# A list scheduler that may leave VectorE and ScalarE idle for work due sooner, and plans with TensorE's clock

## The chip, the core and the metric

The kernel runs on one core of a Trainium2 chip. The metric is the device time of one execution in microseconds (us); less is better. Inputs, outputs and weights are float32 and lie in HBM; the program reads 598 MB and writes 2 MB. The core has five engines with a queue of instructions each: TensorE (PE in the profile) multiplies matrices, VectorE (DVE) and ScalarE (ACT) work element by element, GpSimd (POOL) does little here, and SyncE (SP) issues the loads. Within an engine instructions run in the order in which the program lists them; between engines they wait for each other through semaphores.

## The reference

Two layers of a transformer trunk over 256 tokens of width 2048. Both layers have the same frame, with `cond = silu(c)`:

```python
mod = (cond @ ada_w[i] + ada_b[i])[:, None, :]
sh1, sc1, g1, sh2, sc2, g2 = jnp.split(mod, 6, axis=-1)
h = _rms_norm(x, ln_mix_g[i]) * (1.0 + sc1) + sh1
# layer 0: y = _mla_mixer(h, ...), layer 1: y = _dsa_mixer(h, ...)
x = x + g1 * y
h = _rms_norm(x, ln_ffn_g[i]) * (1.0 + sc2) + sh2
x = x + g2 * _swiglu(h, ffn_w_gate_up[i], ffn_w_down[i])
```

The first mixer, MLA, has low-rank projections with a norm inside them, 16 heads with rotary embedding and a norm of each head's q and k, causal softmax attention and an output projection. The second, DSA, has full q, k and v projections, an indexer that selects 64 keys per query, and attention over those. The FFN has a hidden width of 5632. A root-mean-square norm is `x * rsqrt(mean(x * x) + eps) * g`.

## The kernel before

**Staging.** The 256 tokens stand as two tiles of 128 rows, `xs[0]` and `xs[1]`, in SBUF for the whole program. All weights are streamed from HBM in tiles of 128 x 1024 floats (0.5 MB), used once. Matrix products keep nearly full float32 precision by splitting each operand in a high and a low part: a weight tile `raw` lands, ScalarE writes its high part `whi`, VectorE writes `wlo = raw - whi`, and `mm3` makes three matmuls of each product into a PSUM tile `acc`. Three buffers each of `whi` and `wlo` and five of `raw` stand between the loads and TensorE, so that TensorE can go on for some microseconds only when VectorE is late with `wlo`.

**Modulation.** `cond @ ada_w` is a product with one row. It runs mostly on VectorE: for each of 16 slices of 128 rows, `ada_tiles` does `acc = raw * cond + acc` (tile names `araw` or `raw`, and `ada`). These are the longest VectorE operations beside `wlo`, and a `Stream` spreads them between the weight loads of whatever stage runs. At the start of the program the first layer's `sc1` and `sh1` are made this way in four chunks, with some of the slices on TensorE, while the input projection of MLA already runs on the chunks that are done.

**Norms.** `sumsq` squares on ScalarE and sums along the row (its elementwise result goes to a tile `junk` that nobody reads), and `rstd` computes the reciprocal root on VectorE as a chain of 11 tiny operations, each of which reads the result of the one before (`rs_h`, `rs_t`, `rs_g`, `rs_p`). `norm_stats` and `norm_group` use it for x (results `nv`, `nr`, `xn`), `lora` for the low-rank norms, and each of the eight head pairs of MLA for its q and k (`v8`, `r8`, printed as `r`). After a pair's chain come on VectorE `k_r` and `qs`, on ScalarE the scaling of `kv`, on TensorE the transposes and the scores, on VectorE the masked row maxima (`prob`, `mx`), on ScalarE the exponentials, on VectorE the reciprocal of the sum, on ScalarE the scaling of `prob`, and on TensorE the transposes of `prob` and the product with v.

**Who sets the order.** No line of the kernel issues directly. Every call is recorded as an `Op` with a duration from the table in `cost`, and `place` orders the whole program: it simulates the five engines (`run`), derives from the simulated schedule a due time for every operation (the time at which TensorE's next use of its result would be delayed), simulates again with these due times as priorities, eight times in all, and keeps the schedule with the shortest simulated span. TensorE keeps the order of the source, less an offset for code under `rec.boost`. `run` is greedy: of the operations that are ready when an engine becomes free it takes the one due first, and an engine is never left idle while any operation is ready. `issue` then lists the program in simulated order, and on the chip each engine follows its list.

**Memory.** `const` tiles live for the whole program. A tile with a tag takes one of the tag's buffers in turn, and its first use waits until the buffer's last holder is done (`link`).

## Time and profile before

| | us |
|---|---|
| median of 3 runs | 2390.15 (2389.46 to 2390.41) |
| the profiled execution | 2388.56 |
| its span from first to last instruction | 2386.8 |
| TensorE busy in it | 2299.2 |
| VectorE busy | 1703.9 |
| ScalarE busy | 1145.9 |

The profiled execution is one run with the profiler on; 1.76 us of it lie outside the span. Times inside the trace count from the span's start. By stages: 0 to about 180 is the start (modulation, first norm, input projection of MLA), to about 350 the MLA heads, to 427 the output projection, then the first FFN to 1178, the DSA mixer to 1639 and the second FFN to the end. TensorE's granted clock is given as a share of 2.4 GHz: 1.00 is that level and 0.50 is 1.2 GHz.

### The profile page before, as it was taken

The page shows a single profiled execution, that of the slowest core. Times are in us where ns is not written, and L with a number is a line of the kernel's source. Part 1 is how long each engine was busy: PE and PEld are TensorE (multiplying, and loading weights), DVE is VectorE, ACT ScalarE, POOL GpSimd, SP SyncE. Part 2 cuts the span into 40 slices and gives each one's busy share as a digit, 9 for nine tenths or more (in the row PEclk, how much of TensorE's full clock was granted, in tenths as well). Part 3 has the DMA queues.
Part 4 walks back from the last instruction along what each step waited for, and adds up shares of the span by engine and source line. Part 5 has one row for each costly group of instructions (what it writes and reads, how often), then busy time and mean ns, then how long its engine had stood idle before and what let it go on. Part 6 is the DMA issues. An engine that isn't in the chain of part 4 may idle for free.

```text
span 2386.8 us, 29405 instructions
## 1 busy us (share of the span) xinstructions
PE 2299.2 (96%) x10394; PEld 1866.2 (78%) x10394; DVE 1703.9 (71%) x2373; ACT 1145.9 (48%) x1740; POOL 31.6 (1%) x93
## 2 busy tenths in 40 slices
PE   6889989799999999999899999998999999999999
PEld 2467768688888888888778888887888888888887
DVE  7768979877787788888789666657676554455455
ACT  2248964644434443444455665655444344434443
POOL 1000000000000000000000000000000000000000
PEclk8889999999999999999999999999999999999999
DMA  9958978788899998999667677655887666666665
GB/s 359 337 181 301 336 259 275 262 301 309 300 322 314 314 309 309 324 306 304 227 203 230 195 227 224 200 177 177 290 280 243 193 192 191 189 193 193 187 190 162
DMA packets 278401, 601.87 MB, mean 252 GB/s; under 512 B 18804, under 2 KB 27088, under 8 KB 277998
## 3 DMA queue, kind: packets, MB, share of 16 engines
q1 hardware_dynamic: 277852, 599.97, 76.3%
q8 instruction: 81, 1.33, 0.2%
q14 instruction: 66, 0.54, 0.1%
q10 hardware_dynamic: 402, 0.04, 0.0%
HBM read 597.84 MB, written 2.10 MB: 251 GB/s over the span
## 4 chain that ended last, share of the span: by engine, by line
PE 85%; DVE 7%; ACT 4%; issue 3%; DMA 1%; SPq 0%; DVEq 0%; ACTq 0%
PE acc L398 78%; PE ms L398 7%; DVE ada L398 2%; DVE wlo L398 2%; ACT whi L398 1%; ACT prob L398 1%; DMA araw<-in_ada_w_dram 1%; ACT junk L398 1%; ACT hT L398 0%; DVE y L398 0%; ACT kv L398 0%; DMA raw<-in_ada_w_dram 0%; DVE hT L398 0%; DVE rs_g L398 0%; DVE hf L398 0%
## 5 line engine op out<-in xcount | busy, mean ns | idle before, releaser
L398 DVE TENSOR_TENSOR wlo<-raw,whi 128x1024 fp32r<-128x1024 f32 (+1 forms) x758 | 919.7, 1214 | 520.2 <-ACT whi L398 517.9
L398 PE MATMUL acc<-whi,hT 128*128 128x512 f32 (+1 forms) x4096 | 1282.0, 391 | 3.2 <-ACT hT L398 2.5
L398 ACT ACTIVATE whi<-raw 128x1024 fp32r<-128x1024 f32 (+1 forms) x758 | 797.8, 1054 | 1006.9 <-PE acc L398 922.2
L398 PEld LDWEIGHTS acc<-whi,hT 128*128 128x128 f32 x4096 | 769.4, 189 | 166.0 <-issue 5.8
L398 PE MATMUL acc<-wlo,hT 128*128 128x512 f32 (+1 forms) x2048 | 801.2, 391 | 3.0 <-DVE wlo L398 2.9
L398 PE MATMUL acc<-whi,oT 128*128 128x512 f32 x1920 | 600.2, 391 | 0.0
L398 PEld LDWEIGHTS acc<-wlo,hT 128*128 128x128 f32 x2048 | 386.4, 189 | 82.8 <-DVE wlo L398 4.8
L398 PEld LDWEIGHTS acc<-whi,oT 128*128 128x128 f32 x1920 | 360.9, 188 | 74.5 <-ACT whi L398 0.4
L398 PE MATMUL acc<-wlo,oT 128*128 128x512 f32 x960 | 375.4, 391 | 3.3 <-DVE wlo L398 3.3
L398 DVE SCALAR_TENSOR_TENSOR ada<-raw,condT,ada 128x1024 f32<-128x1024 f32 (+1 forms) x256 | 310.6, 1214 | 43.8 <-DMA raw<-in_ada_w_dram 41.6
L398 PEld LDWEIGHTS acc<-wlo,oT 128*128 128x128 f32 x960 | 180.7, 188 | 41.4 <-DVE wlo L398 4.5
L398 DVE SCALAR_TENSOR_TENSOR ada<-araw,condT,ada 128x512 f32<-128x512 f32 (+1 forms) x176 | 165.6, 941 | 11.6 <-ACT condT L398 6.7
L398 ACT ACTIVATE hT<-ms,modT,modT 128x256 fp32r<-128x256 f32 x64 | 33.8, 568 | 58.3 <-PE ms L398 31.7
L398 PE MATMUL ms<-ident,xn 128*128 128x128 f32 x144 | 29.3, 354 | 25.1 <-DVE rs_p L398 13.0
L398 PE MATMUL ms<-araw,condT 128*1 128x512 f32 x96 | 51.4, 675 | 1.7 <-ACT condT L398 1.7
L398 PEld LDWEIGHTS ms<-ident,xn 128*128 128x128 f32 x144 | 23.3, 189 | 30.2 <-ACT xn L398 12.3
L398 DVE TENSOR_TENSOR y<-acc,gB 128x512 f32<-128x512 f32 x64 | 42.1, 683 | 6.2 <-PE acc L398 6.2
L398 ACT ACTIVATE oT<-ms 128x512 fp32r<-128x512 f32 x60 | 35.7, 598 | 20.6 <-PE ms L398 18.2
L398 DVE TENSOR_TENSOR oT<-ms,oT 128x512 fp32r<-128x512 f32 x60 | 39.7, 683 | 7.4 <-ACT oT L398 7.3
L398 POOL MEMSET ada<- 128x1024 f32 (+1 forms) x30 | 23.6, 785 | 1388.4 <-PE ms L398 702.6
L398 ACT ACTIVATE prob<-prob,mx,qs 128x128 f32<-128x128 f32 (+1 forms) x64 | 34.2, 536 | 13.6 <-DVE mx L398 13.6
L398 DVE TENSOR_TENSOR x<-x,y 128x512 f32<-128x512 f32 x56 | 38.0, 684 | 0.4
(213 smaller groups left out, 995.9 us busy)
## 6 DMA issues: line engine op xcount, KB each, us to landing
raw<-in_ffn_w_gate_up_dram SPq DMA_DIRECT2D x352, 512.0 KB
raw<-in_ada_w_dram SPq DMA_DIRECT2D x240, 512.0 KB
raw<-in_ffn_w_down_dram SPq DMA_DIRECT2D x176, 512.0 KB
araw<-in_ada_w_dram SPq DMA_DIRECT2D x144, 512.0 KB
raw<-in_dsa_w_in_dram SPq DMA_DIRECT2D x114, 512.0 KB
raw<-in_mla_w_out_dram SPq DMA_DIRECT2D x32, 512.0 KB
raw<-in_dsa_w_out_dram SPq DMA_DIRECT2D x32, 512.0 KB
raw<-in_mla_w_in_dram SPq DMA_DIRECT2D x16, 512.0 KB
```

The source lines that it names most:

```text
L398: op.call(*[real(a) for a in op.args], **{k: real(v) for k, v in op.kw.items()})
```

## The change

Five edits. (1) `run` may pass over a ready operation on VectorE or ScalarE. If the operation that it would start now has a rival that becomes ready within 260 ns, and also within 0.4 of this operation's own duration, and is due more than 500 ns sooner, then the engine stays idle until the rival is ready. (2) The simulated TensorE gets a clock: an operation takes its columns at 1.2 GHz if fewer than 3072 columns streamed in the simulated tick before (`pace`). (3) The elementwise result of `sumsq` has three buffers in place of one. (4) To make room, `vrows` moves into a buffer of the tag `hf`, which the rotary angles use too. (5) The rotary tables of MLA get tagged buffers, which `score` and `smask` of the second layer take over when the tables are done. Instructions and bytes are the same; the order of the lists differs nearly everywhere.

```diff
--- before.py
+++ after.py
@@ -309,6 +309,27 @@
     return follow
 
 
+TICK = 10240 / 3.0
+
+
+def pace(op, t, streamed):
+
+    n = elems(op.args[0])
+    cols = 4.0 * n if op.kind != "transpose" and op.args[1].tile.dtype != F32R else 2.0 * n if op.kind == "transpose" else n
+    if op.kind == "strips":
+        cols = 2048.0
+    k = int(t / TICK)
+    hold = op.hold
+    if k and streamed.get(k - 1, 0.0) < 3072:
+        hold = max(hold, cols / 1.2)
+    after = int((t + hold) / TICK)
+    part = 1.0 if after == k else ((k + 1) * TICK - t) / hold
+    streamed[k] = streamed.get(k, 0.0) + part * cols
+    if after != k:
+        streamed[after] = streamed.get(after, 0.0) + (1.0 - part) * cols
+    return hold
+
+
 def run(ops, follow, prio):
 
     left = [len(op.deps) + sum(1 for s in op.order if s not in op.deps) for op in ops]
@@ -322,6 +343,7 @@
         if not left[op.seq]:
             heapq.heappush(later[op.eng], (0.0, prio[op.seq], op.seq))
     chan = 0.0
+    streamed = {}
     done = []
     while len(done) < len(ops):
         best = None
@@ -340,9 +362,18 @@
         while later[e] and later[e][0][0] <= t:
             _, p, s = heapq.heappop(later[e])
             heapq.heappush(now[e], (p, s))
+        p, s = now[e][0]
+        if e in PATIENCE and later[e] and later[e][0][0] < t + PATIENCE[e]:
+            soon = [x for x in later[e] if x[0] < t + min(PATIENCE[e], PATIENT * ops[s].hold) and x[1] < p - MARGIN]
+            if soon:
+                free[e] = min(soon)[0]
+                continue
         op = ops[heapq.heappop(now[e])[1]]
         op.start = t
-        op.end = free[e] = t + op.hold
+        hold = op.hold
+        if e == "PE":
+            hold = pace(op, t, streamed)
+        op.end = free[e] = t + hold
         if op.kind == "dma":
             chan = max(chan, t + DMA_FIRST) + op.bytes / DMA_RATE
             op.seen = chan + DMA_LAST
@@ -360,6 +391,10 @@
 
 
 PASSES = 8
+
+PATIENCE = {"DVE": 260.0, "ACT": 260.0}
+PATIENT = 0.4
+MARGIN = 500.0
 
 
 def place(rec):
@@ -452,7 +487,7 @@
     condT = const.tile([P, NK], F32, name="condT")
     S.activation(condT, pc[:, 0:16], AF.Silu)
 
-    vrows = const.tile([P, P], F32, name="vrows")
+    vrows = sb.tile([P, P], F32, tag="hf", name="vrows")
     G.memset(vrows, 0.0)
     vT = const.tile([P, P], F32, name="vT")
     lnT = {("mix", 0): 0, ("mix", 1): 16, ("ffn", 0): 32, ("ffn", 1): 48}
@@ -647,7 +682,7 @@
         V.scalar_tensor_tensor(out_ap, p, 1.875, y, op0=ALU.add, op1=ALU.mult)
 
     def sumsq(src, n, acc_ap):
-        j = sb.tile([P, 512], mybir.dt.bfloat16, tag="junk", name=nm("junk"), bufs=1)
+        j = sb.tile([P, 512], mybir.dt.bfloat16, tag="junk", name=nm("junk"), bufs=3)
         S.activation(j[:, 0:n], src, AF.Square, accum_out=acc_ap)
 
     def mm3(ps, xh, xl, wh, wl, start, stop):
@@ -789,10 +824,13 @@
             V.tensor_scalar(u, u, -3.1415925, 3.1415925, op0=ALU.max, op1=ALU.min)
             S.activation(cs[:, i], u, AF.Sin)
 
-    def rope_table(name, half, gcol):
-
-        a = const.tile([P, 2, 2 * half], F32, name=name + "A")
-        b = const.tile([P, 2, 2 * half], F32, name=name + "B")
+    def rope_table(name, half, gcol, home=None):
+
+        if home is None:
+            a = const.tile([P, 2, 2 * half], F32, name=name + "A")
+            b = const.tile([P, 2, 2 * half], F32, name=name + "B")
+        else:
+            a, b = (home[:, i * 128:(i + 1) * 128].rearrange("p (t d) -> p t d", t=2) for i in range(2))
         step = 32 // half
         for tt in range(2):
             cc, ss = cos[:, tt, ::step], sin[:, tt, ::step]
@@ -986,8 +1024,8 @@
     ada_src[0] = "hT"
     ones_r = const.tile([P, P], F32R, name="ones_r")
     V.tensor_copy(ones_r, ones)
-    tabq = rope_table("mq", 32, 0)
-    tabk = rope_table("mk", 32, 64)
+    tabq = rope_table("mq", 32, 0, const.tile([P, 384], F32, tag="tabq", name="tabq"))
+    tabk = rope_table("mk", 32, 64, const.tile([P, 384], F32, tag="tabk", name="tabk"))
 
     with rec.boost(HP):
         def lora(banks, gT):
@@ -1185,7 +1223,7 @@
     ikT = const.tile([P, T], F32, name="ikT")
     V.tensor_copy(ikT, pk2[:, 0:T])
 
-    score = const.tile([P, 384], F32, name="score")
+    score = const.tile([P, 384], F32, tag="tabq", name="score")
     V.tensor_copy(score, cmask)
     rng = (slice(0, 128), slice(128, 384))
     for ib in range(2):
@@ -1214,7 +1252,7 @@
                 V.scalar_tensor_tensor(score[:, rng[tt]], rl[:, rng[tt]], iw[:, tt, ib * 8 + h:ib * 8 + h + 1],
                                        score[:, rng[tt]], op0=ALU.mult, op1=ALU.add)
 
-    smask = const.tile([P, 384], F32, name="smask")
+    smask = const.tile([P, 384], F32, tag="tabk", name="smask")
     for tt in range(2):
         for it in range(TOPK // 8):
             m8 = st.tile([P, 8], F32, tag="m8", name=nm("m8"))
```

Below are three places of the order, before and after. Each row is an instruction as it stands in its engine's list; L398 and L433 are the same line of `issue`, and the number in a name counts instructions.

VectorE, the chain of the last head pair in MLA (`rs_h` is its first row, `r_707` its last; `ada` and `wlo` are the long operations of other work). Before, its second half:

```order
L398 SCALAR_TENSOR_TENSOR rs_t_3084<-rs_g_3103,rs_t_3084 128x8
L398 SCALAR_TENSOR_TENSOR ada_2713<-araw_2997,condT,ada_2713 128x1024
L398 TENSOR_TENSOR oT_3167<-ms_3131,oT_3156 128x512
L398 TENSOR_TENSOR rs_g_3103<-rs_t_3084 128x8
L398 SCALAR_TENSOR_TENSOR ada_2713<-araw_3007,condT,ada_2713 128x1024
L398 TENSOR_TENSOR rs_g_3103<-rs_g_3103,rs_h_3065 128x8
L398 SCALAR_TENSOR_TENSOR ada_2713<-araw_3024,condT,ada_2713 128x1024
L398 TENSOR_SCALAR rs_p_3193<-rs_g_3103 128x8
L398 SCALAR_TENSOR_TENSOR ada_2713<-araw_3049,condT,ada_2713 128x1024
L398 TENSOR_TENSOR wlo_3203<-raw_2983,whi_3191 128x1024
L398 TENSOR_TENSOR rs_p_3193<-rs_p_3193,rs_g_3103 128x8
L398 SCALAR_TENSOR_TENSOR r_707_3211<-rs_p_3193,rs_t_3084 128x8
```


After, the whole chain:

```order
L433 TENSOR_SCALAR rs_h_2982<-v_694_2932 128x8
L433 TENSOR_TENSOR mx_2954<-mx_2954,qs_2908 128x4
L433 TENSOR_SCALAR rs_t_2986<-rs_h_2982 128x8
L433 TENSOR_SCALAR rs_t_2986<-rs_t_2986 128x8
L433 TENSOR_TENSOR rs_g_2993<-rs_t_2986 128x8
L433 TENSOR_TENSOR rs_g_2993<-rs_g_2993,rs_h_2982 128x8
L433 SCALAR_TENSOR_TENSOR rs_t_2986<-rs_g_2993,rs_t_2986 128x8
L433 TENSOR_TENSOR rs_g_2993<-rs_t_2986 128x8
L433 TENSOR_TENSOR rs_g_2993<-rs_g_2993,rs_h_2982 128x8
L433 TENSOR_SCALAR rs_p_3007<-rs_g_2993 128x8
L433 TENSOR_TENSOR rs_p_3007<-rs_p_3007,rs_g_2993 128x8
L433 SCALAR_TENSOR_TENSOR r_707_3014<-rs_p_3007,rs_t_2986 128x8
```


Before, the 11 small operations of the whole chain stand among 11 `ada` and `wlo` operations and 4 others, over 26 rows; after, they stand together in 12 rows, with one `mx` of the pair before between them.

VectorE, the norm ahead of the second layer's FFN, from the sum of the second token tile's squares (`nv`) on. Before:

```order
L398 TENSOR_REDUCE nv_13987<-ssq 128x1
L398 TENSOR_TENSOR rs_g_14005<-rs_t_13992 128x1
L398 TENSOR_SCALAR rs_h_14009<-nv_13987 128x1
L398 TENSOR_TENSOR rs_g_14005<-rs_g_14005,rs_h_13990 128x1
L398 TENSOR_TENSOR wlo_14012<-raw_13930,whi_13996 128x1024
L398 TENSOR_SCALAR rs_t_14016<-rs_h_14009 128x1
L398 SCALAR_TENSOR_TENSOR rs_t_13992<-rs_g_14005,rs_t_13992 128x1
L398 SCALAR_TENSOR_TENSOR ada_13470<-raw_13967,condT,ada_13470 128x1024
L398 TENSOR_SCALAR rs_t_14016<-rs_t_14016 128x1
L398 TENSOR_TENSOR rs_g_14005<-rs_t_13992 128x1
L398 TENSOR_TENSOR rs_g_14024<-rs_t_14016 128x1
L398 TENSOR_TENSOR rs_g_14005<-rs_g_14005,rs_h_13990 128x1
```


After, the same stretch:

```order
L433 TENSOR_REDUCE nv_13985<-ssq 128x1
L433 TENSOR_TENSOR rs_g_14000<-rs_g_14000,rs_h_13988 128x1
L433 TENSOR_SCALAR rs_h_14007<-nv_13985 128x1
L433 TENSOR_SCALAR rs_p_14009<-rs_g_14000 128x1
L433 TENSOR_SCALAR rs_t_14011<-rs_h_14007 128x1
L433 TENSOR_TENSOR rs_p_14009<-rs_p_14009,rs_g_14000 128x1
L433 TENSOR_SCALAR rs_t_14011<-rs_t_14011 128x1
L433 SCALAR_TENSOR_TENSOR nr_14015<-rs_p_14009,rs_t_13990 128x1
L433 TENSOR_TENSOR rs_g_14017<-rs_t_14011 128x1
L433 TENSOR_SCALAR xn_14019<-x_270,nr_14015 128x512
L433 TENSOR_TENSOR rs_g_14017<-rs_g_14017,rs_h_14007 128x1
L433 SCALAR_TENSOR_TENSOR rs_t_14011<-rs_g_14017,rs_t_14011 128x1
```


Before, a `wlo` and an `ada` stand between the links of the two token tiles' chains; after, neither is among these rows, nor among the next ones up to the first five `xn`.

SP, the loads at the start, around the second half of x (the second `in_x_dram` row). Before:

```order
L398 DMA araw_241<-in_ada_w_dram 128x2x512
L398 DMA araw_266<-in_ada_w_dram 128x2x512
L398 DMA araw_277<-in_ada_w_dram 128x2x512
L398 DMA ada_254<-in_ada_b_dram 1x512
L398 DMA araw_291<-in_ada_w_dram 128x2x512
L398 DMA x_302<-in_x_dram 128x2048
L398 DMA araw_306<-in_ada_w_dram 128x2x512
L398 DMA araw_321<-in_ada_w_dram 128x2x512
L398 DMA raw_334<-in_mla_w_in_dram 128x2x512
L398 DMA araw_337<-in_ada_w_dram 128x2x512
L398 DMA araw_355<-in_ada_w_dram 128x2x512
L398 DMA raw_369<-in_mla_w_in_dram 128x2x512
```


After:

```order
L433 DMA araw_327<-in_ada_w_dram 128x2x512
L433 DMA araw_338<-in_ada_w_dram 128x2x512
L433 DMA araw_346<-in_ada_w_dram 128x2x512
L433 DMA araw_349<-in_ada_w_dram 128x2x512
L433 DMA araw_359<-in_ada_w_dram 128x2x512
L433 DMA x_373<-in_x_dram 128x2048
L433 DMA raw_379<-in_mla_w_in_dram 128x2x512
L433 DMA ada_371<-in_ada_b_dram 1x512
L433 DMA araw_393<-in_ada_w_dram 128x2x512
L433 DMA raw_401<-in_mla_w_in_dram 128x2x512
L433 DMA raw_411<-in_mla_w_in_dram 128x2x512
L433 DMA raw_420<-in_mla_w_in_dram 128x2x512
```


Before, the second half of x stands behind 17 `araw` tiles, one `raw` tile and the first half of x (1 MB each half); after, behind 24 `araw` tiles and the first half, with the first `raw` tile behind it.

## Rows read from the trace of the kernel before

**Rows 1.** The page, busy us of TensorE (share of span).

```profile
PE 2299.2 (96%) x10394; PEld 1866.2 (78%) x10394; DVE 1703.9 (71%) x2373; ACT 1145.9 (48%) x1740; POOL 31.6 (1%) x93
```

**Rows 2.** Windows: stretch, length, busy us (instructions) per engine, clock, DMA, GB/s.

```profile
0.00:180.00 180.00, 140.88 (x515) 81.00 (x516) 126.72 (x296) 56.71 (x103) 9.82 (x59) 0.89 0.84 292
30.00:60.00 30.00, 21.02 (x72) 10.53 (x71) 28.58 (x102) 9.80 (x19) 1.05 (x2) 0.83 1.05 386
180.00:480.00 300.00, 271.12 (x1300) 222.73 (x1299) 263.36 (x500) 207.12 (x484) 10.25 (x22) 0.95 0.83 287
```

**Rows 3.** Windows, sum over 480 to 1170, 1210 to 1630, 1660 to 2380.

```profile
sum 1830.00, PE 1828.99 PEld 1514.99 DVE 1252.35 ACT 842.30 POOL 11.49; mean PE 609.66 PEld 505.00 DVE 417.45 ACT 280.77 POOL 3.83
```

**Rows 4.** Windows, sum over 1170 to 1210 and 1630 to 1660.

```profile
sum 70.00, PE 56.07 PEld 45.95 DVE 59.24 ACT 39.74 POOL 0.00; mean PE 28.04 PEld 22.98 DVE 29.62 ACT 19.87 POOL 0.00
```

**Rows 5.** Waits of TensorE: us in total, times, longest us.

```profile
PE ms L398 <- DVE ada L398: 21.4, 5, 8.1
PE ms L398 <- DVE rs_p L398: 13.0, 2, 6.9
...
PE ms L398 <- ACT prob L398: 10.9, 6, 4.8
PE ms L398 <- ACT xn L398: 10.9, 2, 8.8
```

**Rows 6.** Timeline of VectorE, 321 to 340: start us, us, operation [idle before].

```profile
321.98 0.13 DVE L398 TENSOR_TENSOR rs_g<-rs_t 128x8 f32<-128x8 f32 x1
322.04 1.27 DVE L398 SCALAR_TENSOR_TENSOR ada<-araw,condT,ada 128x1024 f32<-128x1024 f32 x1
...
333.88 0.17 DVE L398 SCALAR_TENSOR_TENSOR r<-rs_p,rs_t 128x8 f32<-128x8 f32 x1
...
338.99 0.29 DVE L398 CUSTOM_DVE_ANT_0 prob<-ms,cmask 128x128 f32<-128x128 f32 x1 [4.40 <-PE ms L398]
```

**Rows 7.** Timeline of TensorE, last two long waits of the attention.

```profile
343.88 1.78 PE L398 MATMUL ms<-ident,prob 128*128 128x128 f32 x6 [3.85 <-ACT prob L398]
...
356.32 0.69 PE L398 MATMUL acc<-wlo,oT 128*128 128x512 f32 x1 [2.21 <-DVE wlo L398]
```

**Rows 8.** Windows, TensorE just after the wait that ends at 343.88.

```profile
343.88:348.27 4.39, 4.38 (x14) 3.33 (x15) 0.00 (x0) 2.02 (x5) 0.00 (x0) 0.50 0.00 0
```

**Rows 9.** Windows, 220 to 420.

```profile
220.00:330.00 110.00, 105.06 (x541) 86.14 (x540) 106.82 (x236) 98.40 (x279) 5.60 (x14) 1.00 0.96 342
330.00:360.00 30.00, 23.07 (x99) 17.86 (x98) 15.66 (x32) 12.83 (x29) 1.07 (x2) 0.83 0.40 139
360.00:420.00 60.00, 58.50 (x262) 48.21 (x261) 57.30 (x73) 27.33 (x35) 1.05 (x2) 1.00 0.79 268
```

**Rows 10.** Timeline of TensorE, first head pair.

```profile
210.85 1.78 PE L398 MATMUL ms<-ident,prob 128*128 128x128 f32 x6 [4.81 <-ACT prob L398]
```

**Rows 11.** Timeline of VectorE, norm ahead of the second layer's FFN.

```profile
1639.69 0.15 DVE L398 TENSOR_REDUCE nv<-ssq 128x1 f32<-128x4 f32 x1
...
1644.28 0.16 DVE L398 SCALAR_TENSOR_TENSOR nr<-rs_p,rs_t 128x1 f32<-128x1 f32 x1
1644.47 1.28 DVE L398 TENSOR_SCALAR xn<-x,nr 128x512 f32<-128x512 f32 x3
```

**Rows 12.** Timeline of VectorE, norm at the head of the second layer.

```profile
1179.62 0.15 DVE L398 TENSOR_REDUCE nv<-ssq 128x1 f32<-128x4 f32 x1
...
1183.32 0.88 DVE L398 TENSOR_SCALAR xn<-x,nr 128x512 f32<-128x512 f32 x2
```

**Rows 13.** Timeline of VectorE, norm ahead of the first layer's FFN.

```profile
422.05 0.15 DVE L398 TENSOR_REDUCE nv<-ssq 128x1 f32<-128x4 f32 x1
...
427.10 0.15 DVE L398 SCALAR_TENSOR_TENSOR nr<-rs_p,rs_t 128x1 f32<-128x1 f32 x1
```

**Rows 14.** Timeline of ScalarE, the second half of x lands.

```profile
35.93 0.63 ACT L398 ACTIVATE junk<-x 128x512 bf16<-128x512 f32 x1 [5.06 <-DMA x<-in_x_dram]
```

**Rows 15.** Timeline of TensorE, first matmul of the MLA input projection.

```profile
49.05 0.50 PE L398 MATMUL acc<-whi,hT 128*128 128x512 f32 x1 [0.33 <-ACT hT L398]
```


## The prediction

> **What bounds the kernel now.** I read the page first: TensorE is busy for 2299.2 of 2386.8 us, 96% [rows 1], so whatever the other engines gain or lose counts only where TensorE waits for them. The windows say where that is. Over 1830 us of the FFNs and the DSA mixer it is busy for 1828.99 [rows 3]; nothing is to be had there. It idles for 39.1 us of the first 180 and for 28.9 us from 180 to 480 [rows 2], and for 13.9 us in the two stretches of 40 and 30 us around the norms of the second layer [rows 4]. The list of waits names what it waits for: 21.4 us in 5 waits for `ada` on VectorE, 13.0 in 2 for `rs_p`, 10.9 in 6 for `prob`, 10.9 in 2 for `xn` [rows 5]. `rs_p` and `xn` are the end of a norm, and `prob` is the attention behind a norm.
>
> The timelines show why these are late. In the last head pair `rs_g` starts at 321.98, and 0.06 us later VectorE begins an `ada` of 1.27 us; the chain's last row starts at 333.88 only [rows 6]. That is 11.90 us for 7 steps of a chain in which a step takes 0.19 us when nothing stands between (`nr` at 1644.28, its reader at 1644.47 [rows 11]). The row maxima start at 338.99 after 4.40 us of idle VectorE [rows 6], and TensorE waits 3.85 us for `prob` [rows 7]. Then it pays again: for the 4.38 us of work after that wait the granted clock is 0.50, the 1.2 GHz level [rows 8]. At 1.00 that work would take 2.19, so 2.19 us are lost with such a wait. A last wait of 2.21 us for `wlo` follows at 356.32 [rows 7], since loads and weight splits had stopped with the row maxima: 330 to 360 has VectorE busy for 15.66 of 30 us and the DMA engines for 0.40 of it [rows 9].
>
> **What the change is worth, step by step.** The sum is made against the profiled execution, 2388.56, which lies 1.59 below the median of the runs.
>
> Last head pair. Its chain stands contiguous after, so those 7 steps take 7 x 0.19 = 1.3 us in place of 11.9. All work behind it moves up, up to the scores, for which TensorE's list keeps other matmuls. If only the wait for `prob` goes, 3.85 are won; with the half clock behind it 6.04; with the wait at 356.32 as well 8.25. I take 8.0: the 2.21 has the same cause, and I leave a little for a remainder. Bounds 3.8 and 9.5 (the last if the wait at 356.32 also cost half clock, say half as much as the other).
>
> First head pair. A wait of 4.81 us for `prob` [rows 10], but ScalarE's part of it (first exponential, the scaling of `kv`) stays where it is, and the list of TensorE has about as many other matmuls there as before. I take 1.0, bounds 0 and 4.8 + 2.2 = 7.0.
>
> Other waits for `prob`. 10.9 - 4.81 - 3.85 = 2.2 us in four waits [rows 5, 7, 10]. All head pairs but one get shorter chains. I take 1.5, bounds 0 and 2.2.
>
> Norm ahead of the second FFN. From the sum of the second token tile's squares at 1639.69 to its first `xn` at 1644.47 are 4.78 us [rows 11]. With no long operation among them, 11 steps of 0.19 and about 0.5 of the other tile's rows make 2.6. Gain 2.2. TensorE waits on the path here, with nothing else to do, so the gain is whole; bounds 1.5 and 2.7. [...]
>
> Norm at the head of the second layer. From 1179.62 to 1183.32 are 3.70 us [rows 12]; one long operation leaves the chain. 3.7 - 2.6 gives 1.1, bounds 0.5 and 1.6.
>
> Norm ahead of the first FFN. `nv` at 422.05, the last `nr` at 427.10, 5.05 us [rows 13], with `ada` among the links. After, one `wlo` of some 1.2 stays between the two chains' rows, and the squares of the last tile go ahead of a `whi` on ScalarE. I take 2.6 + 0.1 for the chain and so a gain of 2.4, bounds 1.2 and 3.0.
>
> Start. x is needed for the first norm. Its second half lands at 35.93 [rows 14], and 13.1 us later the first `acc` matmul starts [rows 15]. After, it stands 6 tiles further back; 0.524 MB at 386 GB/s [rows 2] are 1.36 us each, so it lands 8.1 us later, at about 44. Four squares and the contiguous chain then need some 3.0 + 2.1 us, and the transposes and `hT` behind them 2.5, so the first `acc` matmul starts near 52, 3 us later. Against it, the `ada` tiles of the first chunks land sooner, and one wait loses its cause. Of the 21.4 us for `ada`, 8.1 are the longest wait, at the first chunk [rows 5]; three of the other four end the later chunks, about 4 us each of the 13.3 left. In the changed list the `wlo` of the next chunk stand behind the last `ada` of the second chunk, so that this wait goes, though not at the next two. Loads, and not TensorE, fill the stage; most of the 3 us and most of that wait are absorbed. I take a gain of 1.0, bounds -5 and 6.
>
> Cost of the patience. A small operation holds VectorE for 0.06 us (321.98 to 322.04 [rows 6]), so a step of 0.19 now leaves it idle for 0.13, ten times in a chain, in 8 pairs: up to 10.4 us, of which some 8 remain, as several chains keep long operations. From 220 to 330 VectorE is busy for 106.82 of 110 us and has 3.2 to spare [rows 9], so 5 us of it lie on what TensorE waits for, if all its slack is used. The `ada` slices that were pushed back (about 7, 8.9 us at 1.27) come in 330 to 420, where 360 to 420 has 2.7 us of spare but 330 to 360 has 14.3 [rows 9]. If none of it fitted, 8.9 - 2.7 = 6.2 would be added. So the cost lies between 0 and 11.2; I take 4.0, nearer to the free end since the 14.3 idle us exist just behind the last chain.
>
> The rest at nothing: `pace` changes plans, not work; the extra `junk` buffers free ScalarE from a wait on its own previous square, which its order already gives; `vrows`, the tables and the mask copy (one small copy in the second layer, whose VectorE is idle for 578 of the 1830 us [rows 3]) are hidden, and if the cover is gone cost under 1 us.
>
> Sum: 8.0 + 1.0 + 1.5 + 2.2 + 1.1 + 2.4 + 1.0 - 4.0 = 13.2. 2388.56 - 13.2 = 2375.4; with 1.59 for the median, **2377**.
>
> **The rivals.** (A) Slower: VectorE becomes the bound in the MLA heads and the output projection. For it speaks 97% busy from 220 to 330 and 57.30 of 60 from 360 to 420 [rows 9]. Then the patience costs its 11.2, `wlo` comes late in three or four lumps, each with 2.2 of half clock (8), and the last pair's 8.0 isn't won, as VectorE's backlog is late there in place of the chain: 9.2 - 11.2 - 8 is a loss of 10, so 2400. It decides from the point where more than 17 us of VectorE's delay reach TensorE. Against it, the idle 14.3 us.
>
> (B) No change: the plan doesn't fit the chip. Waits of 0.13 us are planned from a table of durations; if the rivals in fact come ready at other moments, VectorE just idles. The norms' 5.7 are won, the last pair's 3.85 and the rest are given back in the patience (4) and the start (5): 5.7 + 3.85 - 9 is a gain of 0.6, so 2389.6. [...] The rows show 0.50 after the wait at 343.88 [rows 8], and no run here shows yet whether it stays so.
>
> (C) More: without the waits the half clock vanishes at the three norms as well, 3 x 2.2 = 6.6, and the wait for `ada` with its half clock, 4.0 + 2.2 = 6.2, goes: 2377 - 12.8 = 2364.
>
> (D) The late x is not absorbed: 8.1 us on TensorE in place of the gain of 1.0, so 2386.
>
> **How the numbers follow.** Chances: the forecast 0.55 (2370 to 2384), A 0.10, B 0.13, C 0.14, D 0.08. What a measurement here can tell from no change is 0.2%, 4.8 us: faster is below 2385.4, slower above 2394.9. Faster takes the forecast, C, half of D and a little of B: 0.76. Same takes the rest of D and most of B: 0.13. Slower is A and a small part of B: 0.11. The range from 2364 to 2393 leaves out most of A and the lower half of C, not quite 0.2; that of the likeliest case alone is 2370 to 2384.
>
> **What would show it.** In the changed kernel's timeline, `rs_h` to `r` of the last pair within 3 us, no wait for `prob` near 340, DMA above 0.8 from 330 to 360, and `wlo` waits no longer in total than before; `nv` to the first `xn` of the second tile in 2.6 us in both norms of the second layer; the first `acc` matmul near 52 and three, not four, long waits for `ada`. The forecast is wrong if waits for `wlo` appear between 220 and 420, if the start's stage ends later than now, or if the last pair waits for `prob` as before though its chain is short.

## The result and the profile after

The changed kernel takes 2369.49 us in the median of four runs (2368.59 to 2371.61), the kernel before 2389.81 in four runs beside them (2387.43 to 2390.41). The ratio is 0.992, with a 95% interval of 0.9908 to 0.9932: about 20 us faster, where 13 were forecast (2377, in a range from 2364 to 2393, and from 2370 to 2384 for the likeliest case, which the result misses by half a microsecond).

The page of the changed kernel, busy us and share of the span (2368.2 us, 18.6 less than before):

```profile
PE 2290.7 (97%) x10394; PEld 1860.1 (79%) x10394; DVE 1717.8 (73%) x2373; ACT 1135.9 (48%) x1740; POOL 31.5 (1%) x93
```

TensorE does the same 10394 matmuls in 8.5 us less than in [rows 1], at a mean granted clock of 0.986 in place of 0.981, so fewer of them run at the lower clock, and its idle time falls from 87.6 to 77.5 us. The two make the 18.6.

To see where, take the moments at which TensorE has run out of work: the start of a row less the idle time ahead of it. Four such rows of the kernel before (timeline of TensorE: start, duration, operation, [idle before <- what ended it]), ahead of the low-rank norms of MLA, of the first FFN's norm, of the second layer's norm and of the second FFN's norm:

```profile
167.28 0.44 PE L398 MATMUL ms<-ident,xn 128*128 128x128 f32 x2 [2.17 <-ACT xn L398]
...
427.26 2.98 PE L398 MATMUL ms<-ident,xn 128*128 128x128 f32 x11 [8.76 <-ACT xn L398]
...
1182.99 0.66 PE L398 MATMUL ms<-ident,xn 128*128 128x128 f32 x2 [6.06 <-DVE rs_p L398]
...
1644.04 0.69 PE L398 MATMUL ms<-ident,xn 128*128 128x128 f32 x2 [6.93 <-DVE rs_p L398]
```

The same four in the changed kernel, and two waits that follow the last:

```profile
166.39 0.44 PE L433 MATMUL ms<-ident,xn 128*128 128x128 f32 x2 [0.24 <-ACT xn L433]
...
410.56 0.69 PE L433 MATMUL ms<-ident,xn 128*128 128x128 f32 x2 [7.72 <-ACT xn L433]
...
1164.01 0.66 PE L433 MATMUL ms<-ident,xn 128*128 128x128 f32 x2 [3.98 <-DVE rs_t L433]
...
1622.49 0.41 PE L433 MATMUL ms<-ident,xn 128*128 128x128 f32 x2 [3.74 <-DVE rs_g L433]
1624.15 3.71 PE L433 MATMUL ms<-ident,xn 128*128 128x128 f32 x18 [1.25 <-DVE xn L433]
1629.29 0.66 PE L433 MATMUL ms<-ident,xn 128*128 128x128 f32 x4 [1.43 <-ACT hf L433]
```

| TensorE out of work ahead of | before | after | shift | gained in this stage |
|---|---|---|---|---|
| the low-rank norms of MLA | 165.11 | 166.15 | +1.0 | -1.0 |
| the first FFN's norm | 418.50 | 402.84 | -15.7 | 16.7 |
| the second layer's norm | 1176.93 | 1160.03 | -16.9 | 1.2 |
| the second FFN's norm | 1637.11 | 1618.75 | -18.4 | 1.5 |
| the end | 2386.8 | 2368.2 | -18.6 | 0.2 |

Nearly all is won between the first two of these moments, 16.7 us, and in two places. The first are the low-rank norms and the 39 matmuls that begin there, up to the first one of 128x384 behind them (windows as in [rows 2]: stretch, length, busy us of TensorE, its weight loads, VectorE, ScalarE, GpSimd, each with its number of instructions, then clock, DMA share, GB/s). Before:

```profile
165.11:178.43 13.32, 10.26 (x39) 8.15 (x39) 8.56 (x25) 6.61 (x16) 0.00 (x0) 0.74 0.87 291
```

After:

```profile
166.15:174.31 8.16, 7.67 (x39) 5.99 (x39) 7.27 (x20) 6.04 (x16) 0.00 (x0) 1.00 0.74 236
```

That is 5.2 us: the chain of the last of these norms takes 2.24 us on VectorE in place of 4.59, with no long operation among its links instead of two, the wait of 2.17 us is 0.24, one of 0.90 behind it is 0.25, and the granted clock stays at 1.00 in place of a mean of 0.74. The second place are the head pairs and the output projection, the next 1085 matmuls. Before:

```profile
178.43:418.50 240.07, 223.34 (x1085) 184.45 (x1083) 213.56 (x410) 170.79 (x429) 7.81 (x19) 0.96 0.84 292
```

After:

```profile
174.31:402.83 228.52, 217.87 (x1085) 181.09 (x1083) 220.87 (x406) 164.04 (x428) 8.32 (x20) 0.99 0.88 314
```

That is 11.5 us. The last head pair's chain there, on VectorE:

```profile
300.73 0.17 DVE L433 TENSOR_SCALAR rs_h<-v 128x8 f32<-128x8 f32 x1
...
302.75 0.17 DVE L433 SCALAR_TENSOR_TENSOR r<-rs_p,rs_t 128x8 f32<-128x8 f32 x1
```

It takes 2.02 us from first to last row, a step 0.20, where [rows 6] had 11.90 for 7 steps. The transposes of `prob` that waited 3.85 us in [rows 7] start without a wait, and in the first pair the wait of 4.81 in [rows 10] is 1.43:

```profile
194.65 0.33 PE L433 MATMUL ms<-ident,prob 128*128 128x128 f32 x1 [1.43 <-ACT prob L433]
...
319.09 1.25 PE L433 MATMUL ms<-ident,prob 128*128 128x128 f32 x6
```

The windows that answer to [rows 9], and one ahead of them:

```profile
180.00:220.00 40.00, 38.54 (x220) 33.98 (x219) 37.07 (x88) 38.95 (x111) 1.23 (x4) 1.00 0.82 270
...
330.00:360.00 30.00, 29.52 (x132) 23.53 (x130) 29.72 (x32) 11.32 (x11) 0.53 (x1) 1.00 1.05 390
360.00:400.00 40.00, 34.26 (x139) 26.04 (x140) 39.49 (x51) 14.52 (x23) 1.05 (x2) 0.96 0.75 255
```

The hole is closed: VectorE is busy for 29.72 us from 330 to 360 in place of 15.66, and the loads run at 390 GB/s instead of 139. Now VectorE has next to no idle time up to 400, and TensorE waits 6.2 us for split weights in the output projection (waits of TensorE from 340 to 403):

```profile
PE acc L433 <- DVE wlo L433: 4.2, 8, 1.7
PE acc L433 <- ACT whi L433: 2.0, 1, 2.0
```

The norms answer to [rows 11] and [rows 12] (VectorE; sum of the second tile's squares, and its first `xn`):

```profile
1162.33 0.16 DVE L433 TENSOR_REDUCE nv<-ssq 128x1 f32<-128x4 f32 x1
...
1164.93 1.28 DVE L433 TENSOR_SCALAR xn<-x,nr 128x512 f32<-128x512 f32 x3
...
1621.00 0.16 DVE L433 TENSOR_REDUCE nv<-ssq 128x1 f32<-128x4 f32 x1
...
1623.61 1.28 DVE L433 TENSOR_SCALAR xn<-x,nr 128x512 f32<-128x512 f32 x3
```

Both take 2.60 and 2.61 us, in place of 3.70 and 4.78. At the start, the second half of x lands where its first square is released, and the first `acc` matmul follows later than in [rows 14, 15]:

```profile
45.80 0.63 ACT L433 ACTIVATE junk<-x 128x512 bf16<-128x512 f32 x1 [10.71 <-DMA x<-in_x_dram]
```

```profile
59.13 0.79 PE L433 MATMUL acc<-whi,hT 128*128 128x512 f32 x1
```

### The profile page after: what moved, and what is told of

It is laid out like the page before. It is cut to its first block, busy times and chain, and to the rows that moved or that the text cites. A ratio compares the mean times of both kernels' runs of the same rounds, so it can differ in the third digit from the quotient of the medians.

```text
span 2368.2 us, 29398 instructions
## 1 busy us (share of the span) xinstructions
PE 2290.7 (97%) x10394; PEld 1860.1 (79%) x10394; DVE 1717.8 (73%) x2373; ACT 1135.9 (48%) x1740; POOL 31.5 (1%) x93
## 4 chain that ended last, share of the span: by engine, by line
PE 86%; DVE 7%; ACT 3%; DMA 2%; issue 2%; DVEq 0%; SPq 0%; ACTq 0%
PE acc L433 80%; PE ms L433 6%; DVE ada L433 3%; DVE wlo L433 1%; DMA araw<-in_ada_w_dram 1%; ACT whi L433 1%; ACT hT L433 1%; ACT junk L433 0%; DVE rs_g L433 0%; ACT prob L433 0%; DVE hf L433 0%; DVE y L433 0%; DMA raw<-in_ffn_w_gate_up_dram 0%; DMA raw<-in_ada_w_dram 0%; ACT hf L433 0%
## 5 line engine op out<-in xcount | busy, mean ns | idle before, releaser
L433 DVE TENSOR_TENSOR wlo<-raw,whi 128x1024 fp32r<-128x1024 f32 (+1 forms) x758 | 919.8, 1215 | 520.3 <-ACT whi L433 518.5
L433 PE MATMUL acc<-whi,hT 128*128 128x512 f32 (+1 forms) x4096 | 1281.2, 391 | 2.7 <-ACT hT L433 2.0
L433 ACT ACTIVATE whi<-raw 128x1024 fp32r<-128x1024 f32 (+1 forms) x758 | 797.7, 1053 | 1003.6 <-PE acc L433 945.0
L433 PEld LDWEIGHTS acc<-whi,hT 128*128 128x128 f32 x4096 | 768.9, 188 | 163.6 <-DVE hT L433 4.5
L433 PE MATMUL acc<-wlo,hT 128*128 128x512 f32 (+1 forms) x2048 | 801.1, 391 | 1.1 <-DVE wlo L433 1.1
L433 PE MATMUL acc<-whi,oT 128*128 128x512 f32 x1920 | 598.5, 391 | 2.0 <-ACT whi L433 2.0
L433 PEld LDWEIGHTS acc<-wlo,hT 128*128 128x128 f32 x2048 | 386.1, 189 | 81.0 <-issue 2.6
L433 PEld LDWEIGHTS acc<-whi,oT 128*128 128x128 f32 x1920 | 361.0, 188 | 76.3 <-ACT whi L433 2.4
L433 PE MATMUL acc<-wlo,oT 128*128 128x512 f32 x960 | 377.0, 393 | 5.2 <-DVE wlo L433 5.1
L433 DVE SCALAR_TENSOR_TENSOR ada<-raw,condT,ada 128x1024 f32<-128x1024 f32 (+1 forms) x256 | 310.5, 1214 | 26.4 <-DMA raw<-in_ada_w_dram 25.1
L433 PEld LDWEIGHTS acc<-wlo,oT 128*128 128x128 f32 x960 | 180.5, 188 | 46.3 <-DVE wlo L433 9.4
L433 DVE SCALAR_TENSOR_TENSOR ada<-araw,condT,ada 128x512 f32<-128x512 f32 (+1 forms) x176 | 165.7, 943 | 10.7 <-ACT condT L433 6.1
L433 PE MATMUL ms<-ident,xn 128*128 128x128 f32 x144 | 27.7, 342 | 28.6 <-DVE xn L433 9.4
L433 PE MATMUL ms<-araw,condT 128*1 128x512 f32 x96 | 50.0, 662 | 4.5 <-ACT condT L433 4.5
L433 ACT ACTIVATE hT<-ms,modT,modT 128x256 fp32r<-128x256 f32 x64 | 33.8, 565 | 42.0 <-PE ms L433 26.0
L433 PEld LDWEIGHTS ms<-ident,xn 128*128 128x128 f32 x144 | 21.6, 178 | 33.7 <-DVE xn L433 10.5
L433 DVE TENSOR_TENSOR y<-acc,gB 128x512 f32<-128x512 f32 x64 | 42.3, 684 | 5.2 <-PE acc L433 5.2
L433 POOL MEMSET ada<- 128x1024 f32 (+1 forms) x30 | 23.5, 784 | 1389.7 <-PE ms L433 757.8
L433 DVE TENSOR_TENSOR oT<-ms,oT 128x512 fp32r<-128x512 f32 x60 | 39.9, 684 | 2.6 <-ACT oT L433 2.6
L433 ACT ACTIVATE prob<-prob,mx,qs 128x128 f32<-128x128 f32 (+1 forms) x64 | 34.3, 538 | 14.1 <-DVE mx L433 14.0
L433 ACT ACTIVATE oT<-ms 128x512 fp32r<-128x512 f32 x60 | 35.6, 597 | 11.2 <-PE ms L433 9.0
L433 DVE TENSOR_TENSOR x<-x,y 128x512 f32<-128x512 f32 x56 | 37.9, 685 | 0.2
```

The source lines that it names most:

```text
L433: op.call(*[real(a) for a in op.args], **{k: real(v) for k, v in op.kw.items()})
```

## The experiments

Each was timed against the kernel before on the same chip in the same rounds. The kernel before had medians from 2388.1 to 2389.5 in these rounds; the changed kernel's 2369.5 is from its own, with 2389.8 for the kernel before. A difference between runs of different rounds is therefore uncertain by up to 1.7 us. The theory at the outset: the gain comes from the chains that patience leaves together. Its rivals: the clock in the plan, the buffers, and the luck of a new order.

**Without patience** (`e1_no_patience`).

```diff
-PATIENCE = {"DVE": 260.0, "ACT": 260.0}
+PATIENCE = {}
```

> The changed kernel with the patience taken out; the clock in the plan, the three buffers and the shared memory stay. Theory (the gain of 20 us comes from the chains that patience leaves together): 2385 to 2393, no better than before, and the last head pairs' chains interrupted by long operations again. Rival (planning with TensorE's clock moves other matmuls behind the waits, and the chains matter little): 2368 to 2378. Second rival (any new order is worth some us either way, by luck): anything from 2375 to 2400, with waits at places that neither edit touches.

Measured 2395.50 (ratio 1.003, 1.0019 to 1.0042): slower than before and than the theory's range, so the other edits alone lose 7 us. The last head pair's chain is long again (VectorE, first and last row, with 10 `ada` and `wlo` between them), and TensorE waits for `prob` behind it:

```profile
316.16 0.17 DVE L433 TENSOR_SCALAR rs_h<-v 128x8 f32<-128x8 f32 x1
...
329.45 0.16 DVE L433 SCALAR_TENSOR_TENSOR r<-rs_p,rs_t 128x8 f32<-128x8 f32 x1
```

```profile
339.50 1.73 PE L433 MATMUL ms<-ident,prob 128*128 128x128 f32 x6 [2.92 <-ACT prob L433]
```

Yet the head pairs and the output projection, the same 1085 matmuls, take only 3.7 us more than in the changed kernel:

```profile
179.68:411.91 232.23, 219.28 (x1085) 181.45 (x1083) 214.12 (x409) 164.38 (x426) 7.80 (x19) 0.99 0.86 302
```

They are 7.8 us faster than in the kernel before, without any patience. Of the 25.5 us by which this run's span exceeds the changed kernel's, 4.9 lie at the low-rank norms, where TensorE waits 1.98 us again, and 16.4 behind the output projection (the table at the end of this section has the stages). Most of the 16.4 is no gain on the kernel before: there the order without patience is 13.5 us slower than the kernel before. So this run alone doesn't refute the second rival, the luck of a new order.

**Patience alone** (`e2_patience_alone`): the changed kernel without the two lines in `run` that call `pace`, and with the buffers and memory of before.

```diff
-        if e == "PE":
-            hold = pace(op, t, streamed)
...
-        j = sb.tile([P, 512], mybir.dt.bfloat16, tag="junk", name=nm("junk"), bufs=3)
+        j = sb.tile([P, 512], mybir.dt.bfloat16, tag="junk", name=nm("junk"), bufs=1)
```

> The kernel before with the patience alone; no clock in the plan, one buffer for squares, memory as before. Theory: 2368 to 2378, most of the 20 us. Rival (the clock in the plan): 2383 to 2392. Second rival (luck of the order): any value, unrelated to that of the run with everything but the patience.

Measured 2377.43 (0.9953, 0.994 to 0.9965): a gain of 11 us, a little over half of the 20, and 8 short of the changed kernel.

**All but the clock** (`e3_no_pace`): only the two `pace` lines taken out.

> The changed kernel without TensorE's clock in the plan. Theory: 2368 to 2376, within 6 us of the changed kernel. Rival (the clock in the plan): 2382 to 2390.

Measured 2372.48 (0.9931, 0.9918 to 0.9945). The clock is worth 3 us here at the medians; the interval overlaps the changed kernel's (0.9908 to 0.9932), so this isn't clear of noise.

**One buffer and the memory of before** (`e4_one_buffer`): only the second half of the diff of `e2_patience_alone`, `pace` stays.

> The changed kernel with one buffer for squares and the memory of before; patience and clock stay. Theory: 2368 to 2374, the buffers cost and bring nothing, as was forecast. Rival (the square of one row waits for the buffer and the plan is built on that): 2376 to 2385.

Measured 2380.11 (0.9966, 0.9953 to 0.9978): the rival's range. The buffers or the memory are worth 10.6 us, which had been forecast at nothing. The squares show why. In the run with one buffer (`e9_junk_one`, next), ScalarE starts one square of 128 columns every 0.42 to 0.44 us:

```profile
300.61 0.30 ACT L433 ACTIVATE junk<-kv 128x128 bf16<-128x128 f32 x1
300.81 0.19 ACT L433 ACTIVATION_READ_ACCUMULATOR junk<-kv 128x1 f32 x1
301.03 0.31 ACT L433 ACTIVATE junk<-kv 128x128 bf16<-128x128 f32 x1
...
301.47 0.31 ACT L433 ACTIVATE junk<-kv 128x128 bf16<-128x128 f32 x1
```

In the changed kernel, with three, every 0.29:

```profile
297.02 0.29 ACT L433 ACTIVATE junk<-kv 128x128 bf16<-128x128 f32 x1
297.22 0.18 ACT L433 ACTIVATION_READ_ACCUMULATOR junk<-kv 128x1 f32 x1
297.31 0.29 ACT L433 ACTIVATE junk<-kv 128x128 bf16<-128x128 f32 x1
...
297.61 0.29 ACT L433 ACTIVATE junk<-kv 128x128 bf16<-128x128 f32 x1
```

With one buffer the next square starts 0.22 us after the read of the sum has begun, with three 0.09. ScalarE's order already put them one behind the other; what one buffer costs comes on top of that.

**One buffer, all else as changed** (`e9_junk_one`).

```diff
-        j = sb.tile([P, 512], mybir.dt.bfloat16, tag="junk", name=nm("junk"), bufs=3)
+        j = sb.tile([P, 512], mybir.dt.bfloat16, tag="junk", name=nm("junk"), bufs=1)
```

> The changed kernel with one buffer for squares; the shared memory, the patience and the clock stay. With one buffer two squares of 128 columns in a row start 0.43 us apart in the kernel before, with three 0.29 us in the changed one. Theory (the wait of a square on the one before it costs ScalarE about 0.14 us, eight times in a head pair, and that is what the memory edits are worth): 2377 to 2382, and the squares 0.43 apart again. Rival (the shared memory moved the loads and the order): 2368 to 2373.

Measured 2377.58 (0.995, 0.9937 to 0.9964). The buffers are worth 8.1 us with patience and clock beside them, and the shared memory at most the small rest.

**Buffers and memory alone** (`e6_buffers_alone`): the changed kernel with `PATIENCE = {}` and without the `pace` lines.

> The kernel before with three buffers for squares and the shared memory, without patience and clock. Theory (ScalarE's saving counts only where the chains are short enough that ScalarE is what TensorE waits for): 2384 to 2390, at most 5 below before, with the last head pair's chain as long as before. Rival (the buffers bring their 8 to 10 us by themselves): 2377 to 2382.

Measured 2387.57 (0.9991, 0.9983 to 1.0): 2 us, if anything. Its squares are 0.29 us apart too, but TensorE still waits 3.85 us for `prob` in the last head pair. Beside the run without patience (2395.50) it says that the clock in the plan, with the buffers and the memory, costs 8 us. By stages it wins 4.1 us in the head pairs and the output projection (236.3 to 232.2) and loses 13.8 behind them. Why it loses there without patience isn't settled.

**Patience on one engine** (`e7_dve_only`, `e8_act_only`).

```diff
-PATIENCE = {"DVE": 260.0, "ACT": 260.0}
+PATIENCE = {"DVE": 260.0}
```

> The changed kernel with patience on VectorE alone. Theory (the chains of reciprocal roots on VectorE are what patience mends): 2367 to 2374. Rival (ScalarE's patience, which keeps long weight splits from standing ahead of the squares and exponentials, carries half of it): 2378 to 2386.

> The changed kernel with patience on ScalarE alone. Theory (VectorE's chains): 2388 to 2398, like the run without patience. Rival (ScalarE's patience carries half): 2378 to 2386.

Measured 2370.81 (0.9922, 0.991 to 0.9934) with VectorE alone, and 2388.77 (0.9995, 0.9986 to 1.0003) with ScalarE alone. VectorE's patience is worth 24.7 of the 26.0 us by itself, and ScalarE's 6.7; they overlap.

**Less work on VectorE** (`e10_less_ada`).

```diff
                 k = t * nk + kk
+                if layer == 0 and c0 in (3 * D + 1024, 4 * D + 1024) and w == 512 and kk == 1:
+                    continue
```

> The changed kernel without 16 of VectorE's modulation operations of 128x512 (about 0.75 us each, 12 us in all) in the last two jobs that run beside the output projection of the first layer; that half of the two modulation sums is left out, the loads stay. Theory (VectorE is what the stage from the head pairs to the end of the output projection is bound by, and what patience won there was VectorE's idle time): 2360 to 2365, with the waits for wlo and whi from 354 to 392 (about 6 us) gone, though no more than these and their half clock. Rival (the stage is bound by TensorE's own work and the order): 2367 to 2371.

Measured 2363.32 (0.9897, 0.9884 to 0.9911), 6.2 us below the changed kernel: of 12 us taken off VectorE about half reach the end. The windows of this run that answer to the last two of the changed kernel:

```profile
330.00:360.00 30.00, 28.14 (x128) 23.00 (x127) 29.82 (x33) 10.88 (x14) 0.53 (x1) 1.00 1.05 389
360.00:400.00 40.00, 34.17 (x150) 26.57 (x148) 32.86 (x45) 15.61 (x22) 1.05 (x2) 1.00 0.80 271
```

VectorE has 7.1 us to spare from 360 to 400, and TensorE is out of work ahead of the first FFN's norm 3.5 us sooner. But the waits did not go, though that had been expected. From 340 to 403 they make 7.0 us (5.2 for `wlo`, 1.8 for other things) where the changed kernel has 6.2. What is shorter is TensorE's busy time, 214.6 in place of 217.9 us in the head pairs and the output projection (the clock from 360 to 400 is 1.00, not 0.96), and the wait at the first FFN's norm, 5.7 in place of 7.7. That VectorE alone bounds this stage isn't shown: from 330 to 360 the DMA engines' share is 1.05 in both runs.

**Additions on GpSimd** (`e12_pool_add`), all computed.

```diff
-        V.tensor_tensor(xb, xb, y, op=ALU.add)
+        (G if layer == 0 and sec == 2 and nb < 3 else V).tensor_tensor(xb, xb, y, op=ALU.add)
```

> The changed kernel with 6 of the 8 additions of the first layer's attention result to x (128x512, 0.68 us each, 4.1 us in all) on GpSimd in place of VectorE; all is computed. Theory (VectorE is the bound there): 2364 to 2368. Rival (GpSimd is so slow at it, or so much in VectorE's way, that nothing is won): 2369 to 2376.

Measured 2374.96 (0.9945, 0.9932 to 0.9957), 5.5 us above the changed kernel. GpSimd takes 2.2 us for one, and some of VectorE's operations take longer meanwhile (GpSimd, then VectorE in the same stretch):

```profile
364.00 2.19 POOL L433 TENSOR_TENSOR x<-x,y 128x512 f32<-128x512 f32 x1 [9.48 <-DVE y L433]
366.15 2.26 POOL L433 TENSOR_TENSOR x<-x,y 128x512 f32<-128x512 f32 x1
```

```profile
363.84 1.22 DVE L433 TENSOR_TENSOR wlo<-raw,whi 128x1024 fp32r<-128x1024 f32 x1
364.97 0.69 DVE L433 TENSOR_TENSOR y<-acc,gB 128x512 f32<-128x512 f32 x1
365.57 1.71 DVE L433 TENSOR_TENSOR wlo<-raw,whi 128x1024 fp32r<-128x1024 f32 x1
367.20 1.76 DVE L433 SCALAR_TENSOR_TENSOR ada<-araw,condT,ada 128x512 f32<-128x512 f32 x1
368.99 0.75 DVE L433 SCALAR_TENSOR_TENSOR ada<-araw,condT,ada 128x512 f32<-128x512 f32 x1
```

The `wlo` that starts ahead of the first addition takes 1.22 us as elsewhere. The next one starts 0.62 us before that addition ends and takes 1.71. The `ada` at 367.20 starts 1.21 us before the second addition ends (368.41) and takes 1.76; the one behind it, 0.75. GpSimd's additions seem held up in turn: both start beside a `wlo` and end 1.13 us after it (366.19 after 365.06, 368.41 after 367.28), and so do two later ones (382.80 after 381.67, 390.15 after 389.02).

**Patience by place** (`e11_from_out_proj`, `e13_up_to_heads`): patience for operations recorded from the output projection on, and for those recorded before it.

```diff
-        if e in PATIENCE and later[e]
+        if e in PATIENCE and s >= FROM[0] and later[e]
...
+    FROM[0] = len(rec.ops)
     ada.rate = 1.0
     out_proj(oT, m_out, 0)
```

> The changed kernel with patience only for operations recorded after the head pairs of MLA (output projection, FFNs, second layer). Theory (five sixths of the gain is won in the start and the head pairs, where eight chains and VectorE's full load meet, and the three later norms are worth 3 us): 2387 to 2394, 2 to 8 below the run without patience. Rival (the three norms, as forecast, are worth 6 us with their half clock and more): 2380 to 2386.

Measured 2380.99 (0.9968, 0.9957 to 0.9979): 14.5 us below the run without patience. The theory that five sixths belong to the start and the heads falls, and the rival's range holds.

> The changed kernel with patience only for operations recorded before the output projection (start and head pairs): the other half of the run that had it only from there on, which took 14.5 of the 26 us between the run without patience and the changed kernel. Theory (each stage's patience is worth what it mends there, and the parts add): 2381 to 2387, that is 2395.5 less the 11.5 us that are left, with 4 us lost again at the two norms of the second layer. Rival (patience in the heads gives nearly all by itself, and what it gives in one place the plan gives back or takes elsewhere): 2370 to 2378. Second rival (the heads' part is worth nothing without the rest): 2390 to 2396.

Measured 2384.29 (0.9978, 0.9969 to 0.9987): 11.2 us below the run without patience. The two halves make 25.7, and all of patience 26.0: they add, as far as rounds can be compared. The rows of TensorE ahead of the first FFN's norm show that the halves aren't cut as the code is. First with patience from the output projection on:

```profile
414.60 0.69 PE L434 MATMUL ms<-ident,xn 128*128 128x128 f32 x2 [9.28 <-ACT xn L434]
```

TensorE is out of work there at 405.32, 6.6 us sooner than without patience (422.13 less a wait of 10.22 makes 411.91), though the head pairs were planned without it. The last pair's chain is whole all the same, 2.03 us long; two others take 2.8 and 3.0 us, and five 10.2 to 11.1 us with 5 to 8 `ada` and `wlo` among their links:

```profile
315.31 0.17 DVE L434 TENSOR_SCALAR rs_h<-v 128x8 f32<-128x8 f32 x1
...
317.34 0.17 DVE L434 SCALAR_TENSOR_TENSOR r<-rs_p,rs_t 128x8 f32<-128x8 f32 x1
```

The due times come from the whole program, in eight passes, so patience behind the heads also changes what is urgent in them. Even so, the head pairs and the output projection take no longer in this run than in the changed kernel, whose chains last 2.0 to 3.8 us, but 3.3 us less:

```profile
180.13:405.32 225.19, 217.18 (x1085) 179.98 (x1083) 216.39 (x410) 164.41 (x427) 7.79 (x19) 0.99 0.90 313
```

**By stages.** Each stage ends where TensorE runs out of work ahead of the next norm, as in the first table, and the second at the first matmul of 128x384 behind the low-rank norms. Each has the same number of matmuls in all runs. All in us, of the profiled execution:

| | start | low-rank norms | pairs and output projection | first FFN | DSA mixer | second FFN |
|---|---|---|---|---|---|---|
| before | 165.1 | 13.3 | 240.1 | 758.4 | 460.2 | 749.7 |
| changed | 166.2 | 8.2 | 228.5 | 757.2 | 458.7 | 749.5 |
| without patience | 166.6 | 13.1 | 232.2 | 766.5 | 462.9 | 752.4 |
| buffers and memory alone | 167.0 | 13.2 | 236.3 | 759.2 | 459.5 | 749.3 |
| one buffer for squares | 164.4 | 8.2 | 238.7 | 754.5 | 459.7 | 749.3 |
| patience on ScalarE alone | 170.4 | 11.9 | 227.0 | 761.1 | 460.5 | 752.5 |
| patience from the output projection on | 167.0 | 13.1 | 225.2 | 763.9 | 461.8 | 748.4 |
| patience up to the heads | 167.2 | 8.2 | 234.4 | 761.1 | 460.2 | 751.9 |

The low-rank norms follow VectorE's patience: 8.0 to 8.2 us in all runs where it covers them, 11.9 to 13.3 where it doesn't. The head pairs and the output projection do not follow it. In the table they are quickest in two runs in which five and seven of the eight chains are long (9 to 14 us), and patience up to the heads, which makes all eight short (2.0 to 4.1 us), leaves them 2.2 us slower than no patience at all. Its 11 us come from the low-rank norms and from the stages behind it, and patience from the output projection on wins 7.0 of its 14 us in the stage that holds the pairs. So it is shown for the whole program that patience on VectorE brings the gain. Through which waits is shown for the low-rank norms, the last head pair and the two norms of the second layer, and not for the other seven pairs.

No run beat the changed kernel with all its work done.

## Why the prediction was right, and where its terms were off

The direction was right, and the mechanism (a chain that stays whole ends a wait of TensorE) is borne out at the last head pair and at the norms of the second layer. That the time is in the range owes something to luck. In the sum, the head pairs with the cost of patience stood for 6.5 us, the three norms for 5.7 and the start for 1.0; in the profiled executions they brought 11.5, 2.9 and -1.0, and 5.2 came from a place without a term.

**The low-rank norms** of MLA were that place. Their wait of 2.17 us is 0.24 in the changed kernel and 0.22 to 0.25 in four runs whose patience covers VectorE there (`e9_junk_one`, `e10_less_ada`, `e12_pool_add`, `e13_up_to_heads`), and the lower clock behind it (0.50 from 169.63 to 175.34, with the 128x512 matmuls 0.43 us apart) is gone: 1.00 from 168.09 to 174.09 in the changed kernel, with these matmuls 0.23 us apart in it and in the four. This is the forecast mechanism where the prediction had not looked.

**The last head pair** went as forecast: a contiguous chain of 2.02 us, no wait for `prob`, the loads without a gap. The waits for `prob` and, behind it, for `wlo` stand where the chain is long (3.85 and 2.21 us before, 2.92 and 2.28 without patience, 3.85 and 1.88 with ScalarE's alone) and no wait for `prob` stands there in any run that has it short. So much is shown. What it is worth to the end isn't: the run with ScalarE's patience alone pays these waits and still passes the pairs and the output projection in 227.0 us, the changed kernel, with 6.2 us of later waits, in 228.5.

**The first head pair** was mis-sized. 1.0 had been taken within 0 and 7.0, with the argument that ScalarE's part stays. The wait fell by 3.4, and the work behind it (4.39 us from 210.85 on) no longer runs at 0.50 (1.00 from 194.65 to 199.00), so 5.6 are won. ScalarE's part did get shorter: before, four scalings of `kv` (1.26 us) and a `whi` (0.83) stood between the last exponential and the scaling of `prob`; now it is one `whi` of 1.04. The other waits for `prob`, put at 1.5 of 2.2 us, brought 0.7: one of 1.5 us is left, at 264.

**The squares** are the step that failed: "the extra `junk` buffers free ScalarE from a wait on its own previous square, which its order already gives". It does not give it. One buffer costs ScalarE 0.14 us for each square that directly follows another, at most 9 us (an estimate) for eight squares in each of eight pairs, on an engine that is busy for 38.95 of 40 us from 180 to 220 in the changed kernel. With patience and clock that is worth 8.1 us. Without the clock the buffers and the memory bring 5.0 with patience (2377.43 to 2372.48) and 1.9 without. That ScalarE is what TensorE waits for only where VectorE's chains no longer hold it up would fit this, but no run shows it. In the run with one buffer the head pairs and the output projection take 10.2 us longer than in the changed kernel, and the other stages give 3.5 of that back:

```profile
172.55:411.25 238.70, 219.57 (x1085) 181.35 (x1083) 224.87 (x411) 168.79 (x427) 7.79 (x19) 0.98 0.86 302
```

Against the kernel before, that run wins 1.4 us there, where 8.0 + 1.0 + 1.5 - 4.0 = 6.5 had been summed. That it measured 2377.58, beside the forecast of 2377, is luck: the 5.2 of the low-rank norms stand in for what the pairs fell short of.

**The cost of patience** was put at 4.0 in bounds of 0 to 11.2, as VectorE's work comes too late in the output projection. TensorE waits 6.2 us for `wlo` and `whi` there now. That VectorE's load is behind these waits is argued from its 39.49 busy us of 40, and not shown: when 12 us of its work were left out, 6.2 us came back at the end, but not from these waits. Rival A had the right place, and not the size. Of the signs that were to prove the forecast wrong, two appeared: 5.1 us of waits for `wlo` between 220 and 420, though the kernel before has 3.3 there too, and a start that ends later.

**The norms of the second layer** were right to 0.01 us in the chains (2.60 and 2.61 for 2.6), but the second FFN's was put too high in the gain. The second FFN's norm brought 0.2 us in place of 2.2. The wait ahead of it fell from 6.93 to 3.74, but waits of 1.25 and 1.43 and two smaller ones follow where before there was one of 0.28 us, since `xn`, `hf` and `hT` of the next columns come no sooner: the first `acc` matmul starts 10.95 us after TensorE ran out of work, before 10.80. Before, TensorE ran that stretch at the lower clock (0.50 from 1644.04 to 1648.50) and was late itself; that it hadn't to wait for this reason is a reading of the rows. With the second layer's norm (1.5 us, for 1.1) and the first FFN's (1.2, for 2.4; its chain, put at 2.7, takes 3.2), 2.9 us were won where 5.7 had been summed. Rival C needed the lower clock to vanish at the norms. It doesn't. The stretches behind the waits at the first FFN's norm, at the second layer's and at the second FFN's:

```profile
410.56:414.00 3.44, 2.84 (x11) 2.33 (x12) 3.33 (x7) 2.93 (x6) 0.00 (x0) 0.50 0.56 158
1164.01:1168.00 3.99, 3.18 (x14) 2.79 (x15) 3.69 (x10) 1.47 (x3) 0.00 (x0) 0.50 0.00 2
1622.49:1627.00 4.51, 3.26 (x16) 3.02 (x16) 3.85 (x13) 1.33 (x3) 0.00 (x0) 0.65 0.00 0
```

**The start** was right that a late x is absorbed, and wrong in how late. x lands at 45.80, near the 44 that were worked out, but the first `acc` matmul comes at 59.13, not 52, since the chain's first row stands on VectorE behind the sum of a modulation job that waits 2.56 us for TensorE, and starts at 54.73. Yet TensorE is out of work at the end of this stage only 1.0 us later than before; a gain of 1.0 had been forecast. Rival D, which charged the 8.1 us in full, is refuted. The wait for `ada` at the end of the second chunk is gone, and those of the next two remain (3.70 at 110.47 and 4.29 at 143.73), as read from the order.

**The clock in the plan** was costed at nothing, as it "changes plans, not work". The plan matters: 8 us are lost by it without patience, and beside the rest 3 are won at the medians. Whether the chip's clock follows the rule in `pace` isn't shown by any run.

## What to carry to other kernels

A planner that always takes ready work put operations of 1.2 to 1.3 us into gaps of 0.13 us of a dependent chain here (11.90 us for 7 steps); one that may idle for a fraction of the long operation's duration gets the chain back (2.02 us for all of it), and the work that is pushed back must be charged where that engine is next full. A shorter chain is worth something only where TensorE has nothing else to do: at the low-rank norms it brought 5.2 us, while the stage of the head pairs was quickest with five of eight chains long. So look for every norm on the path before you price the longest chain. A scratch buffer that nobody reads still orders its writers (squares 0.42 to 0.44 us apart with one buffer, 0.29 with three): give repeated small operations on a busy engine more than one. And cost a gain at a wait only up to the next operand that is late behind it: two chains that came out at their forecast length here brought 1.7 us together where the chains alone said 3.3.
